# Attention's instructions queued behind the last product's eviction, and loads, splits and softmax given other priorities, in a hybrid encoder layer

## The chip, the cores and the metric

One core of one Trainium2 chip. The metric is the time of one execution in microseconds (us); three runs of the kernel before gave a median of 2874.46, from 2874.05 to 2876.97.

The core's engines each execute their own instructions in program order and wait for each other by semaphores: TensorE (PE; weight loads are listed apart as PEld), VectorE (DVE), ScalarE (ACT), GpSimd (POOL) and SyncE (SP). All loads and stores of this kernel are issued by SP, one after the other: an issue that has to wait, for its tile to come free or for the data that it stores, holds back every later issue.

## The reference

One layer on 2048 tokens of width 1024, in float32. Three mixers read the same normalised input; their outputs are projected, gated, added and projected again; an MLP follows.

```python
h = rmsnorm(x, g_mix)
z = h @ w_in                       # 1024 x 5648
qk_m, v_m, o_m, i_pre, f_pre, qkv_na, q_mem, gate_pre = jnp.split(z, split_idx, axis=-1)
...
h_m = ...    # bidirectional chunkwise mLSTM on qk_m (after a short convolution), v_m, gated by o_m
h_na = neighbourhood_attention(q_na, k_na, v_na, rpb)       # 8 heads, windows of 8 x 16 on a 32 x 64 grid
h_mem = memory_cross_attention(q_mem, rmsnorm(mem, g_mem), w_mem_kv, ...)   # 256 memory tokens, 4 heads
gates = jax.nn.sigmoid(gate_pre).reshape(bsz, s, 3, 1024)
y = gates[:, :, 0] * (h_m @ w_proj_mlstm) + gates[:, :, 1] * (h_na @ w_proj_na) \
    + gates[:, :, 2] * (h_mem @ w_proj_mem)
x = x + y @ w_out
return x + jnp.square(jax.nn.relu(rmsnorm(x, g_ffn) @ w_up)) @ w_down
```

Both attentions are a softmax over scores: the neighbourhood's scores get a bias (rpb) added, the memory's do not.

## The kernel before

**Products.** Every float32 operand of a large product is split in two parts, hi and lo, and each product is three matmuls, hi x hi, hi x lo and lo x hi (`mm3`, lines L240, L241 and L242). A product of 128 x 512 outputs over 1024 inputs is 8 x 3 = 24 matmuls into one PSUM bank (`tok_group` with tokens on the partitions, `ch_group` with channels there). ScalarE then moves the bank to SBUF; this is called the eviction here (L513, L528, L536, L548, L573, L616, L688 for the seven kinds of product). Phases 1 and 2 have two PSUM banks, tag `mm`, for products, so a product can begin only when the eviction of the one before the last is done. The attentions have three banks `tr` for transposes and three `mx` for scores and values.

**Phases.** Phase 1 goes over four blocks of 512 tokens (`block_a`). Each block computes q and k of the neighbourhood attention (`naqk`), q and k of the mLSTM, v of the neighbourhood attention and q of the memory attention (`navm`), v, for blocks 2 and 3 the 24 tiles of the branch gates, and o. At the end of block 3, hT, the split and normalised input, is loaded again with that of another block: three loads of a quarter (L580) and eight loads of parts of the last quarter (L584). Phase 2 uses it for the gates left over (`late_gates`, the first of them in two pieces, columns 0 to 383 and 384 to 511) beside the mLSTM. Phase 3 does the projections and the MLP.

**Streams.** Between the matmuls of a product, at every second step, `tick` runs one step of the jobs (transposes and splits of the next block's input, stores) and of each stream: the two attentions in phase 1, the mLSTM in phase 2. A step issues a handful of instructions: neighbourhood scores (L1094), bias and minimum (L1098), Exp (L1100), transposes (L1114) and their copies to npt (L1117 on ScalarE, L1119 on VectorE), values (L1128) and their split into nho (L1134, L1135); memory scores (L1246), maximum (L1249), Exp (L1253), transposes (L1265), copy to mpT (L1267).

**Order.** TensorE's order is as written in the program. On the other engines a scheduler picks, among the instructions whose inputs it takes to be ready, by priority: program order, shifted where the code changes `cur_priority`. A larger value goes later. Constants: LOW = 100, LATER = 60, SOON = 40. `issue_after(ins)` makes what is issued inside it come after `ins` in this order.

**Weights.** `fetch` loads a weight unit of 512 KB into one of three raw tiles (L181) and splits it, hi on ScalarE (L184) and lo on VectorE (L185), into one of five split tiles; all of it is shifted later by 60. Other loads and stores are issued at their place in the program: tiles of x (L473; two tiles, which the sums of w_down, L596, also use), q and k of the neighbourhood attention (L1048, L1049), its v (L1078, L1079), its bias (L1085, four tiles), stores (L105).

**Input.** `prep_x` scales a tile of the transposed input by eight VectorE instructions (L428), `split_part` splits it into hT (L445 on ScalarE, L446 on VectorE). In block 0 the input is transposed on TensorE and split at L361 and L362.

## Time and profile before

| what | value |
| --- | --- |
| median of three runs | 2874.46 us |
| profiled execution, its own time | 2875.37 us |
| its span in the trace | 2873.7 us |
| mean granted TensorE clock | 0.998 |
| TensorE waits in the span for neighbourhood scores, for memory Exps | 3.5 us, two times |
| TensorE wait for the first split input | 3.0 us, once |
| TensorE wait for an eviction of v | 1.8 us, once |
| DMA moved | 631.70 MB |

A row of a timeline has start in us, duration in us, engine, line, operation, output <- input by the program's names, shapes and types, count; in brackets the engine's idle time before it and what ended that. A row of the waits has the total in us, the number of waits, the longest. A row of the windows has the stretch, its length, the busy time of each engine asked for with its instructions in brackets, the granted clock (1.00 is full speed), the mean share of the DMA engines that is busy, and GB/s. In the rows of a window with all engines the order is PE, PEld, DVE, ACT, POOL.

### The profile page before, as it was taken

To read this page: it belongs to the slowest core of one execution; us is meant where nothing else is said; L and a number is where in the kernel's file an instruction comes from. 1 tells how busy PE (TensorE), PEld (TensorE's weight loads), DVE (VectorE), ACT (ScalarE), POOL (GpSimd) and SP (SyncE) were. 2 spreads that over 40 slices of the span, in tenths; PEclk is the share of its full clock that TensorE was granted. 3 is DMA by queue.
4 is the path that set the end of the run, shared out by engine and by line. 5 is a ranking of instruction groups with operands and counts; after the bars stand their busy time and mean duration, and the time that the engine had idled before them with its cause. 6 is when DMAs were issued, how large, how long until landed. Compare 5 with 4: busy or idle time off the path is not lost.

```text
span 2873.7 us, 41503 instructions
## 1 busy us (share of the span) xinstructions
PE 2852.6 (99%) x14950; PEld 2358.5 (82%) x14950; DVE 2042.3 (71%) x3518; ACT 1173.5 (41%) x2209; POOL 195.7 (7%) x254
## 2 busy tenths in 40 slices
PE   8999999999999999999999999999999999999999
PEld 7878788888888888888888888888788888888887
DVE  6676775577665545747699888866786998887666
ACT  7465654454544443532243334433312433343332
POOL 4121210011000112310000000000000000000000
PEclk9999999999999999999999999999999999999999
DMA  8686778877899888978444446756773444476553
GB/s 294 189 267 212 223 239 262 263 233 233 258 311 311 274 258 272 310 249 283 134 144 150 161 147 239 255 191 223 260 218 122 154 143 157 157 249 229 194 188 137
DMA packets 345149, 631.70 MB, mean 220 GB/s; under 512 B 29584, under 2 KB 151376, under 8 KB 344944
## 3 DMA queue, kind: packets, MB, share of 16 engines
q1 hardware_dynamic: 344944, 629.06, 66.8%
q8 instruction: 118, 1.93, 0.3%
q14 instruction: 87, 0.71, 0.1%
HBM read 452.32 MB, written 176.62 MB: 219 GB/s over the span
## 4 chain that ended last, share of the span: by engine, by line
PE 97%; DVE 1%; issue 1%; ACT 1%; DMA 0%; POOL 0%; SPq 0%; ACTq 0%; DVEq 0%; POOLq 0%
PE mm L240 29%; PE mm L242 29%; PE mm L241 29%; PE tr L1114 2%; PE mx L1128 1%; PE pn L890 1%; PE mx L1094 1%; PE pn L893 1%; PE mx L899 1%; PE mx L1275 1%; PE tr L1265 1%; PE mx L1246 0%; DVE ws L185 0%; PE mx L864 0%; PE tr L965 0%
## 5 line engine op out<-in xcount | busy, mean ns | idle before, releaser
L240 PE MATMUL mm<-X,ws 128*128 128x512 f32 x896 | 349.4, 390 | 0.0
L241 PE MATMUL mm<-X,ws 128*128 128x512 f32 x896 | 348.6, 389 | 0.0
L242 PE MATMUL mm<-X,ws 128*128 128x512 f32 x896 | 348.6, 389 | 0.0
L185 DVE TENSOR_TENSOR ws<-wr,ws 128x1024 fp32r<-128x1024 f32 (+2 forms) x195 | 238.9, 1231 | 133.9 <-ACT ws L184 131.8
L240 PE MATMUL mm<-hT,ws 128*128 128x512 f32 (+1 forms) x776 | 307.7, 397 | 0.7 <-ACT ev L573 0.7
L242 PE MATMUL mm<-hT,ws 128*128 128x512 f32 (+1 forms) x776 | 302.0, 389 | 0.0
L241 PE MATMUL mm<-hT,ws 128*128 128x512 f32 (+1 forms) x776 | 301.7, 389 | 0.0
L184 ACT ACTIVATE ws<-wr 128x1024 fp32r<-128x1024 f32 (+2 forms) x195 | 204.5, 1054 | 168.8 <-PE mm L242 116.3
L242 PE MATMUL mm<-X 128*128 128x512 f32 x616 | 239.7, 389 | 0.5 <-DVE X L1533 0.5
L240 PE MATMUL mm<-X 128*128 128x512 f32 x616 | 239.7, 389 | 0.1
L241 PE MATMUL mm<-X 128*128 128x512 f32 x616 | 239.6, 389 | 0.0
L240 PE MATMUL mm<-ws,hT 128*128 128x512 f32 (+2 forms) x640 | 232.9, 364 | 4.9 <-ACT hT L361 3.0
L210 ACT ACTIVATE ws<-wr 128x512 fp32r<-128x512 f32 x224 | 133.8, 627 | 232.4 <-PE mm L242 145.8
L242 PE MATMUL mm<-ws,hT 128*128 128x512 f32 (+2 forms) x640 | 224.9, 351 | 0.4 <-DVE hT L362 0.4
L241 PE MATMUL mm<-ws,hT 128*128 128x512 f32 (+2 forms) x640 | 224.2, 350 | 0.8 <-DVE ws L185 0.8
L1532 ACT ACTIVATE X<-X 128x1024 fp32r<-128x1024 f32 x109 | 115.7, 1062 | 213.4 <-DMA X<-s_s 96.0
L240 PEld LDWEIGHTS mm<-X,ws 128*128 128x128 f32 x896 | 168.2, 188 | 35.4 <-issue 0.5
L241 PEld LDWEIGHTS mm<-X,ws 128*128 128x128 f32 x896 | 168.2, 188 | 35.3 <-issue 0.5
L242 PEld LDWEIGHTS mm<-X,ws 128*128 128x128 f32 x896 | 168.2, 188 | 34.8
L1533 DVE TENSOR_TENSOR X<-X 128x1024 fp32r<-128x1024 f32 x109 | 132.1, 1222 | 62.1 <-ACT X L1532 61.5
L1549 DVE TENSOR_TENSOR acc<-acc,mm 128x512 f32<-128x512 f32 x192 | 126.3, 683 | 69.5 <-PE mm L242 69.4
L240 PEld LDWEIGHTS mm<-hT,ws 128*128 128x128 f32 x776 | 146.1, 188 | 31.6 <-issue 4.3
(280 smaller groups left out, 5953.6 us busy)
## 6 DMA issues: line engine op xcount, KB each, us to landing
wr<-in_w_units_dram SPq DMA_DIRECT2D x289, 512.0 KB
s_s<-u SPq DMA_DIRECT2D x32, 1024.0 KB
s_g<-ev SPq DMA_DIRECT2D x96, 256.0 KB
ev<-s_g SPq DMA_DIRECT2D x96, 256.0 KB
s_a<-u SPq DMA_DIRECT2D x96, 256.0 KB
X<-s_s SPq DMA_DIRECT2D x45, 512.0 KB
nab<-in_rpb_dram SPq DMA_DIRECT2D x96, 220.0 KB
xt<-in_w_units_dram SPq DMA_DIRECT2D x32, 512.0 KB
```

The costliest lines, as they stand in the source:

```text
L184: nc.scalar.activation(w[:, 0, ks], raw[:, ks], AF.Copy)
L185: nc.vector.tensor_tensor(w[:, 1, ks], raw[:, ks], w[:, 0, ks].bitcast(F32), ALU.subtract)
L210: nc.scalar.activation(hi, src, AF.Copy)
L240: mm(out, lhs[0], rhs[0], start=first, stop=False)
L241: mm(out, lhs[0], rhs[1], start=False, stop=False)
L242: mm(out, lhs[1], rhs[0], start=False, stop=last)
L890: mm(pn[h % 2][:, h // 2], pt[:, h], v1[:, h], start=h < 2, stop=first)
L893: mm(pn[h % 2][:, h // 2], qw[hp, h // 2], C[hp, h // 2], start=False, stop=True)
L1114: nc.tensor.transpose(ptp[0:120, j], sb[:, j * 120:(j + 1) * 120], self.ident)
L1532: nc.scalar.activation(hi, src, AF.Copy)
L1533: nc.vector.tensor_tensor(lo, src, hi.bitcast(F32), ALU.subtract)
L1549: nc.vector.tensor_tensor(c, first[t] if first else c, p, ALU.add)
```

## The change

Five edits, all on order:

- Each eviction is noted in `self.out`, and `tick` runs the streams inside `queued(self.out)`: what a stream issues comes after the last eviction written so far, on every engine that the scheduler orders. `behind`, used by the mLSTM, is now a call of the same helper.
- In `mem_unit` maximum and Exp are moved 40 earlier (`sooner()`).
- In `split_part` both halves of the split are moved 100 later (`sooner(-LOW)`).
- In `fetch` the load is issued at its place in the program; only the splits stay 60 later.
- The loads of q, k, v and bias of the neighbourhood attention are moved 100 earlier.

```diff
--- before.py
+++ after.py
@@ -89,7 +89,7 @@
         self.streams, self.qkq, self.memq, self.aux_end = [], [], [], False
         self.na_ready, self.na_end, self.na_rate, self.tk = [], False, 1, 0
         self.na_v, self.na_vfree = [], 2
-        self.jobs = []
+        self.jobs, self.out = [], ()
         self.wplan, self.wready = self.plan(), []
 
 
@@ -113,11 +113,12 @@
         f = self.jobs.pop(0) if self.jobs else None
         if f:
             f()
-        for g in list(self.streams):
-            try:
-                next(g)
-            except StopIteration:
-                self.streams.remove(g)
+        with self.queued(self.out):
+            for g in list(self.streams):
+                try:
+                    next(g)
+                except StopIteration:
+                    self.streams.remove(g)
         self.tk = (self.tk + 1) % 4
 
     def drain(self):
@@ -174,11 +175,11 @@
         w = w[:, :2 * n].rearrange("p (k l c) -> p l k c", k=nk, l=2)
         src = self.a["w_units"][i] if i < first else self.a["w_navm"][i - first]
         raw, src = (x.rearrange("p (k c) -> p k c", k=nk) for x in (raw, src))
-        prio = self.tc.cur_priority
-        self.tc.cur_priority = prio + self.later
         for k0 in range(0, nk, nk // parts):
             ks = slice(k0, k0 + nk // parts)
             nc.sync.dma_start(raw[:, ks], src[:, ks])
+        prio = self.tc.cur_priority
+        self.tc.cur_priority = prio + self.later
         for k0 in range(0, nk, nk // parts):
             ks = slice(k0, k0 + nk // parts)
             nc.scalar.activation(w[:, 0, ks], raw[:, ks], AF.Copy)
@@ -442,8 +443,9 @@
         nc = self.nc
         hi = dst[:, 0, 4 * g:4 * g + 4, t * 128:(t + 1) * 128]
         lo = dst[:, 1, 4 * g:4 * g + 4, t * 128:(t + 1) * 128]
-        nc.scalar.activation(hi, p, AF.Copy)
-        nc.vector.tensor_tensor(lo, p, hi.bitcast(F32), ALU.subtract)
+        with self.sooner(-LOW):
+            nc.scalar.activation(hi, p, AF.Copy)
+            nc.vector.tensor_tensor(lo, p, hi.bitcast(F32), ALU.subtract)
 
     def rms_x(self, b):
 
@@ -510,7 +512,7 @@
                 self.mem_rms()
             p = self.tok_group(hT, w, t)
             z = self.t("zna", [128, 512], 4)
-            nc.scalar.activation(z, p, AF.Copy)
+            self.out = nc.scalar.activation(z, p, AF.Copy).ins,
             self.qkq.append(self.na_qk(b, t, z.rearrange("p (a b) -> p a b", b=32)))
         if b + 1 < NB:
             rms = self.rms_x(b + 1)
@@ -525,7 +527,7 @@
         for t in range(4):
             p = self.tok_group(hT, w, t, slice(0, 256), 4)
             s = self.ev()[:, 0:256]
-            nc.scalar.activation(s, p, AF.Copy)
+            self.out = nc.scalar.activation(s, p, AF.Copy).ins,
 
             for half in range(2):
                 for r in range(2):
@@ -533,8 +535,8 @@
                     self.store(self.scr["vna"][half, 8 * b + 2 * t + r], s[p0:p0 + 40])
             p = self.tok_group(hT, w, t, slice(256, 528), 4)
             z = self.t("zm", [128, 256], 4)
-            nc.vector.tensor_copy(z, p[:, 0:256])
-            nc.scalar.activation(zif[:, t], p[:, 256:272], AF.Copy)
+            v = nc.vector.tensor_copy(z, p[:, 0:256])
+            self.out = v.ins, nc.scalar.activation(zif[:, t], p[:, 256:272], AF.Copy).ins
             self.memq.append(self.mem_unit(b, t, z))
         for g in {0: [0], 1: [1, 2], 2: [3, 4], 3: [5, 6, 7]}[b]:
             self.na_ready.append(g)
@@ -545,7 +547,7 @@
                 self.prep_x()
             p = self.tok_group(hT, w, t)
             s = self.ev()
-            nc.scalar.activation(s, p, AF.Copy)
+            self.out = nc.scalar.activation(s, p, AF.Copy).ins,
             self.store(self.scr["v"][b][t * 128:(t + 1) * 128], s)
             if b == NB - 1 and t % 2 == 0:
                 sums = sums or self.sums_down(15)
@@ -570,7 +572,7 @@
                 self.prep_x()
             p = self.tok_group(hT, w, t)
             s = self.ev()
-            nc.scalar.activation(s, p, AF.Tanh, scale=0.5)
+            self.out = nc.scalar.activation(s, p, AF.Tanh, scale=0.5).ins,
             nc.vector.scalar_tensor_tensor(s, s, 1.0, gml, ALU.add, ALU.mult)
             self.store(self.scr["og"][b][t * 128:(t + 1) * 128], s)
             if b == NB - 1:
@@ -613,7 +615,7 @@
 
         p = self.ch_group(w or self.take(1)[0], hT or self.hT, cuts)
         s = self.ev()
-        self.nc.scalar.activation(s, p, AF.Tanh, scale=0.5)
+        self.out = self.nc.scalar.activation(s, p, AF.Tanh, scale=0.5).ins,
         self.store(self.scr["gate"][b][j], s)
 
     def late_gates(self, more):
@@ -685,7 +687,7 @@
         self.n += 1
         z = self.p_a.tile([128, TB + 6], F32, name=f"cz_{self.n}", tag="cz", bufs=3)
         nc.vector.tensor_copy(z[:, 0:4], self.halo[:, c])
-        nc.scalar.activation(z[:, 4:4 + TB], p, AF.Copy)
+        self.out = nc.scalar.activation(z[:, 4:4 + TB], p, AF.Copy).ins,
         if last:
             nc.vector.memset(z[:, 4 + TB:], 0.0)
         else:
@@ -796,12 +798,22 @@
             self.rows[d, b] = dict(em=em, ac=ac)
 
     @contextlib.contextmanager
-    def behind(self):
+    def queued(self, marks):
 
         with contextlib.ExitStack() as stack:
-            for ins in self.marks:
+            for ins in marks:
                 stack.enter_context(self.tc.issue_after(ins))
             yield
+
+    def behind(self):
+        return self.queued(self.marks)
+
+    @contextlib.contextmanager
+    def sooner(self, n=SOON):
+
+        self.tc.cur_priority -= n
+        yield
+        self.tc.cur_priority += n
 
     def ml_chunk(self, d, c):
 
@@ -1043,10 +1055,11 @@
         qs = self.scr["qs"][:, g, hg].rearrange("(h d) l f t -> d h l (f t)", d=32)
         ks = self.scr["ks"][:, hg, :, kr0 * 64:(kr0 + nr) * 64].rearrange("(h d) l t -> d h l t", d=32)
 
-        for i, (lq, lk) in enumerate(((0, 0), (0, 1), (1, 0))):
-            ds = slice(32 * i, 32 * i + 32)
-            nc.sync.dma_start(q[ds].bitcast(F32), qs[:, :, lq])
-            nc.sync.dma_start(k[ds, :, :nr * 64].bitcast(F32), ks[:, :, lk])
+        with self.sooner(LOW):
+            for i, (lq, lk) in enumerate(((0, 0), (0, 1), (1, 0))):
+                ds = slice(32 * i, 32 * i + 32)
+                nc.sync.dma_start(q[ds].bitcast(F32), qs[:, :, lq])
+                nc.sync.dma_start(k[ds, :, :nr * 64].bitcast(F32), ks[:, :, lk])
         return q, k
 
     def na_unit(self, g, hg, half, before, wait):
@@ -1075,14 +1088,16 @@
         vt = self.p_a.tile([120, 4, 128], F32, name=f"nav{g}_{hg}_{half}", tag="nav", bufs=2)
         src = self.scr["vna"][half, kr0:kr0 + nr, :, hg * 128:(hg + 1) * 128].rearrange("r k c -> (r k) c")
         nf = nr // 3
-        nc.sync.dma_start(vt[:, :nf], src[:nf * 120].rearrange("(j p) c -> p j c", p=120))
-        nc.sync.dma_start(vt[:nr % 3 * 40, nf], src[nf * 120:])
+        with self.sooner(LOW):
+            nc.sync.dma_start(vt[:, :nf], src[:nf * 120].rearrange("(j p) c -> p j c", p=120))
+            nc.sync.dma_start(vt[:nr % 3 * 40, nf], src[nf * 120:])
         u["vt"] = vt
 
     def na_bias(self, u, h):
         bias = self.p_a.tile([128, 440], F32, name=f"nab{u['g']}_{u['hg']}_{u['half']}_{h}", tag="nab", bufs=NAB)
         pat = {0: 1, 7: 2}.get(u["g"], 0)
-        self.nc.sync.dma_start(bias[:, :u["nk"]], self.a["rpb"][pat, u["half"], u["hg"] * 4 + h, :, :u["nk"]])
+        with self.sooner(LOW):
+            self.nc.sync.dma_start(bias[:, :u["nk"]], self.a["rpb"][pat, u["half"], u["hg"] * 4 + h, :, :u["nk"]])
         u["bias"].append(bias)
 
     def na_scores(self, u, h):
@@ -1245,12 +1260,12 @@
                     js = slice(j * 64, j * 64 + 64)
                     nc.tensor.matmul(psc[j][:, p], q[js, lq, p], self.mk[js, lk, p], start=i == 0, stop=i == 2)
         for j in range(2):
-            nm = self.small(2, "m")
-            nc.vector.tensor_reduce(nm, psc[j], AX.X, ALU.max, negate=True)
-            sm = self.small(2, "m")
+            nm, sm = self.small(2, "m"), self.small(2, "m")
             e = self.t("me", [128, 2, 256], 4)
-            for p in range(2):
-                nc.scalar.activation(e[:, p], psc[j][:, p], AF.Exp, bias=nm[:, p:p + 1], accum_out=sm[:, p:p + 1])
+            with self.sooner():
+                nc.vector.tensor_reduce(nm, psc[j], AX.X, ALU.max, negate=True)
+                for p in range(2):
+                    nc.scalar.activation(e[:, p], psc[j][:, p], AF.Exp, bias=nm[:, p:p + 1], accum_out=sm[:, p:p + 1])
             rs = self.small(2, "m")
             nc.vector.reciprocal(rs, sm)
             nc.vector.tensor_tensor(e, e, rs.unsqueeze(2).to_broadcast([128, 2, 256]), ALU.mult)
```

How the order of instructions moves, at three places. A row is line, operation, output <- input, shape; x2 is a repeat. The line numbers of the changed kernel are up to 15 larger than those of before for the same instruction.

ScalarE at the third v product of block 0: me and sm are the memory softmax, mpT its transposed copy, nsb the neighbourhood scores, ev a product's tile for the store, mm its bank. Before:

```order
L608 ACTIVATE ev_152_1395<-tr_151_1390,bif_421 16x512
L1253 ACTIVATE me_157_1416,sm_156_1415<-mx_153_1399,sm_155_1413 128x256 x2
L1253 ACTIVATE me_161_1425,sm_160_1424<-mx_154_1400,sm_159_1422 128x256 x2
L1267 ACTIVATE mpT_167_1462<-tr_166_1457 128x512
L1100 ACTIVATE nsb1_429,sm_170_1486<-nsb1_429,sm_169_1484 128x320
L548 ACTIVATE ev_163_1437<-mm_150_1371 128x512
L548 ACTIVATE ev_172_1491<-mm_165_1450 128x512
```

Now:

```order
L1268 ACTIVATE me_157_1415,sm_156_1414<-mx_153_1399,sm_155_1413 128x256 x2
L1268 ACTIVATE me_161_1424,sm_160_1423<-mx_154_1400,sm_159_1422 128x256 x2
L550 ACTIVATE ev_163_1437<-mm_150_1371 128x512
L1282 ACTIVATE mpT_167_1462<-tr_166_1457 128x512
L1115 ACTIVATE nsb1_429,sm_170_1486<-nsb1_429,sm_169_1484 128x320
L185 ACTIVATE ws_131_1264<-wr_131_1263 128x2x512
L550 ACTIVATE ev_172_1491<-mm_165_1450 128x512
```

The eviction of mm_150 moved from behind the copy of mpT and the neighbourhood's Exp to ahead of both; the eviction of the next product, mm_165, stays behind them.

SP at the end of phase 1: the third load of a quarter of hT, the load of weight wr_1774 and the stores of the last o products. Before:

```order
L580 DMA hT_213<-s_hT1_157 128x16x128
L105 DMA s_o3_91<-ev_1779_10515 128x512
L580 DMA hT_213<-s_hT1_157 128x16x128
L105 DMA s_o3_91<-ev_1781_10545 128x512
L181 DMA wr_1774_10439<-in_w_units_dram 128x1024
L584 DMA hT_213<-s_hT1_157 128x2x128 x3
L105 DMA s_o3_91<-ev_1783_10575 128x512
L584 DMA hT_213<-s_hT1_157 128x2x128 x5
```

Now:

```order
L105 DMA s_o3_91<-ev_1779_10515 128x512
L582 DMA hT_213<-s_hT1_157 128x16x128
L180 DMA wr_1774_10439<-in_w_units_dram 128x1024
L105 DMA s_o3_91<-ev_1781_10545 128x512
L582 DMA hT_213<-s_hT1_157 128x16x128
L105 DMA s_o3_91<-ev_1783_10575 128x512
L586 DMA hT_213<-s_hT1_157 128x2x128 x8
```

The weight's load moved ahead of the third quarter of hT and of the store that preceded both; the eight part loads moved behind the last store.

VectorE at the gates of block 3: nho is the split of the neighbourhood's values, npt a copy of transposed scores, xt the tiles of the w_down sums, ws a weight's split. Before:

```order
L1135 TENSOR_TENSOR nho_1602_9547<-mx_1694_10015,nho_1602_9547 128x4x32
L1119 COPY npt_1696_10037<-tr_1695_10033 120x384
L1106 MEMSET nsb1_429 128x40
L1098 ISA nsb1_429,sm_1698_10041<-mx_1697_10039,nab7_1_0_0_9917 128x320
L1098 ISA sm_1698_10041 128x1
L185 TENSOR_TENSOR ws_1660_9822<-wr_1660_9821,ws_1660_9822 128x8x128
L1102 RECIPROCAL sm_1700_10045<-sm_1699_10043 128x1
L1103 TENSOR_SCALAR nsb1_429<-nsb1_429,sm_1700_10045 128x320
L1106 MEMSET nsb2_430 128x40
L1098 ISA nsb2_430,sm_1704_10071<-mx_1703_10069,nab7_1_0_1_9962 128x320
```

Now:

```order
L598 TENSOR_TENSOR xt_1659_9819<-xt_1659_9819,xt_1658_9817 128x512
L1134 COPY npt_1713_10110<-tr_1712_10106 120x384
L598 TENSOR_TENSOR xt_1659_9819<-xt_1659_9819 128x512
L1121 MEMSET nsb0_428 128x40
L598 TENSOR_TENSOR xt_1658_9817<-xt_1658_9817,xt_1659_9819 128x512
L598 TENSOR_TENSOR xt_1658_9817<-xt_1659_9819,xt_1658_9817 128x512
L186 TENSOR_TENSOR ws_1660_9822<-wr_1660_9821,ws_1660_9822 128x8x128
L1150 TENSOR_TENSOR nho_1602_9547<-mx_1694_10015,nho_1602_9547 128x4x32
L1113 ISA nsb2_430,sm_1704_10071<-mx_1703_10069,nab7_1_0_1_9962 128x320
```

The split of nho_1602 moved behind a copy that belongs to a later head, four sums of w_down and a weight's split; the scores' minimum of sm_1704 follows it as before. On ScalarE at the same place the Exp into sm_1705, which reads that minimum, now stands directly ahead of the gate's eviction ev_1707; before it stood behind it.

## The prediction

> **What bounds the kernel now.** I read the page's busy times and chain first, then the table of what TensorE waits for, then timelines around those waits.
>
> ```profile
> span 2873.7 us, 41503 instructions
> PE 2852.6 (99%) x14950; PEld 2358.5 (82%) x14950; DVE 2042.3 (71%) x3518; ACT 1173.5 (41%) x2209; POOL 195.7 (7%) x254
> PE 97%; DVE 1%; issue 1%; ACT 1%; DMA 0%; POOL 0%; SPq 0%; ACTq 0%; DVEq 0%; POOLq 0%
> ...
> PE mx L1094 <- ACT me L1253: 3.5, 2, 1.8
> PE mm L240 <- ACT hT L361: 3.0, 1, 3.0
> PE mm L240 <- ACT ev L548: 1.8, 1, 1.8
> ```
>
> TensorE is busy 99% of the span and 97% of the chain. The change leaves its instructions and their order alone, so the time can move only by TensorE's idle time (columns of the wait rows: us in total, times, longest) and by the clock that idling costs. What a reordering can win in phases 1 and 2 is mainly these waits, 8.3 us in all or 0.3%; what it can lose is not bounded by a row, since every wait that is hidden now can come out. So I took each wait and each place where the order of an in-order engine or of the one DMA queue (SP) changes, and asked who gets late. The profiled execution took 2875.37 us, 0.9 above the median 2874.46 of the three runs; I work out differences on its trace and add them to the median.
>
> **Term A, the eviction behind an attention Exp (gain).** Third v product of block 0:
>
> ```profile
> 124.80 0.56 ACT L1100 ACTIVATE nsb<-nsb,sm 128x320 f32<-128x320 f32 x1 [4.08 <-DVE sm L1098]
> 125.36 1.06 ACT L548 ACTIVATE ev<-mm 128x512 f32<-128x512 f32 x2
> ...
> 125.99 0.67 PE L240 MATMUL mm<-ws,hT 128*128 128x512 f32 x1 [1.76 <-ACT ev L548]
> ...
> 119.40:122.80 3.40, 3.40 (x19) 1.00 0.33 118
> 122.80:126.20 3.40, 1.64 (x8) 0.99 0.11 19
> 126.20:129.60 3.40, 3.40 (x11) 0.51 0.75 248
> ```
>
> ScalarE stood 4.08 us for the Exp's input while the eviction, ready long before, was queued behind it; the next matmul waited 1.76. Now the eviction stands ahead of the Exp (first order listing), so 1.8 goes. The window rows (length, TensorE busy with its matmuls, granted clock, DMA) show a second price: the 3.4 us after the stall ran at 0.51, 11 matmuls instead of 19, which loses 0.49 x 3.4 = 1.7. A = -3.4; bounds -1.8 (the clock would have dropped anyway) and -3.4.
>
> The Trainium skill, "TensorE: Matmul & The Clock Gate", section "Why this matters for your kernels", asks for no idle gap above about 3 us and says that one idle window brings half clock. By it the 1.76 us stall would have cost no clock, A would be -1.8 and the whole sum 1.7 slower; the row with 0.51 speaks against that.
>
> **Term B, memory Exps first (gain).** The two waits of L1094 for L1253 are the 3.5 us above. Ahead of the second one's Exps ScalarE had
>
> ```profile
> 312.41 0.60 ACT L513 ACTIVATE zna<-mm 128x512 f32<-128x512 f32 x1
> 312.90 0.59 ACT L1117 ACTIVATE npt<-tr 120x512 f32<-120x512 f32 x1
> 313.38 0.63 ACT L952 ACTIVATE sq<-zna 128x512 f32<-128x512 f32 x1
> ```
>
> 1.8 us that the Exps now precede, so nearly the whole wait (I take 1.6) can go. At the first, the reduction of the memory unit before it now stands on VectorE behind eight gain multiplications (2.2 us, term C) and a weight split (1.2), which can cost what the earlier Exps win; I count that wait as unchanged. B = -1.6; bounds -3.5 (both go) and 0.
>
> **Term C, the bias load ahead of stores (loss).** The o product of block 2, where SP must bring one weight in time:
>
> ```profile
> 582.62 0.62 DVE L1098 CUSTOM_DVE_ANT_0 nsb<-mx,nab 128x440 f32<-128x440 f32 x1 [1.49 <-PE mx L1094]
> ...
> 569.66 0.38 SPq L473 DMA_DIRECT2D xt<-in_xT_dram  x1
> 573.85 2.19 DVE L428 SCALAR_TENSOR_TENSOR xt<-xt,gmix,gbc 128x128 f32<-128x128 f32 x8 [0.92 <-DMA xt<-in_xT_dram]
> ...
> 584.94 0.43 SPq L181 DMA_DIRECT2D wr<-in_w_units_dram  x1
> 591.77 1.04 ACT L184 ACTIVATE ws<-wr 128x1024 fp32r<-128x1024 f32 x1
> 592.84 1.23 DVE L185 TENSOR_TENSOR ws<-wr,ws 128x1024 fp32r<-128x1024 f32 x1 [0.25 <-ACT ws L184]
> 594.12 0.50 PE L241 MATMUL mm<-ws,hT 128*128 128x512 f32 x1 [0.76 <-DVE ws L185]
> ```
>
> The bias nab4_0_0_0 takes the tile that the L1098 at 582.62 reads, so it cannot issue before 583.2. It now stands ahead of two s_t3 stores, an x tile that must wait until such a store has landed (two x tiles in all), and this weight's load. A transfer of that size took 4.2 us (569.66 to 573.85): 583.6 + 0.5 + 4.2 = 588.3 for the x tile, 588.7 for the weight, 3.7 later than 584.94. The weight had landed by 591.77; if it took between 4.2 and 6.8 us it lands between 592.9 and 595.5 now, and its two splits (2.27) end between 595.2 and 597.8, against 594.12. That is +1.1 to +3.7 beyond the 0.76 that is there. C = +2.2, near the middle; bounds 0 (the L1098 comes sooner) and +3.7.
>
> **Term D, low work ahead of a due operation (loss).** Gates of block 3:
>
> ```profile
> 878.71 0.49 PE L1114 MATMUL tr<-ident,nsb 128*120 128x128 f32 x3
> 879.70 0.55 DVE L1119 COPY npt<-tr 120x384 f32<-120x384 f32 x1
> L596 DVE TENSOR_TENSOR xt<-xt,xt 128x512 f32<-128x512 f32 x48 | 32.4, 685 | 14.5 <-DMA xt<-in_w_units_dram 14.0 <-issue 0.2
> 872.52 0.29 DVE L1135 TENSOR_TENSOR nho<-mx,nho 128x128 fp32r<-128x128 f32 x1 [1.93 <-ACT nho L1134]
> 876.18 0.49 DVE L1098 CUSTOM_DVE_ANT_0 nsb<-mx,nab 128x320 f32<-128x320 f32 x1
> ...
> 876.77 0.56 ACT L1100 ACTIVATE nsb<-nsb,sm 128x320 f32<-128x320 f32 x1
> 875.71 0.60 ACT L616 ACTIVATE ev<-mm 128x512 f32<-128x512 f32 x1 [0.68 <-PE mm L242]
> ...
> 882.16 0.40 PE L1094 MATMUL mx<-nak,naq 96*128 96x320 f32 x1
> 882.40 0.40 PE L240 MATMUL mm<-hT,ws 128*128 128x512 f32 x1
> ```
>
> In the new order (third listing) VectorE does the copy of npt_1713, which needs the transposes that end at 879.2, then three w_down sums (L596), the split of ws_1660, and only then L1135, which ran at 872.52 before. 879.2 + 0.5 + 3 x 0.65 + 1.2 + 0.3 = 883.1. TensorE's scores at 882.16 use the PSUM bank that L1135 frees: 1.0 late. Behind L1135 come L1098, the Exp and, on ScalarE behind that Exp, the eviction of ev_1707: 883.1 + 0.4 + 0.56 + 0.6 = 884.7, needed at 882.40 + 1.0 = 883.4, another 1.3. D = +2.3; bounds 1.0 (the first wait alone) and 2.8 (the copy at 879.70, as before).
>
> **Term E, the reload of the normalised input (loss).** Start of phase 2:
>
> ```profile
> 921.31 0.55 SPq L580 DMA_DIRECT2D hT<-s_hT  x1
> ...
> 926.75 0.53 SPq L580 DMA_DIRECT2D hT<-s_hT  x1
> ...
> 930.46 0.33 SPq L181 DMA_DIRECT2D wr<-in_w_units_dram  x1
> ...
> 926.00:927.00 1.00, 1.00 (x6) 0.82 (x5) 0.00 (x0) 0.24 (x1) 0.00 (x0) 1.00 0.72 264
> 927.00:928.00 1.00, 1.00 (x6) 0.83 (x5) 0.61 (x1) 0.36 (x1) 0.00 (x0) 1.00 0.02 8
> ...
> 932.85 0.44 PE L240 MATMUL mm<-hT,ws 128*128 128x384 f32 x1 [0.69 <-ACT ev L573]
> ...
> 30.60:34.00 3.40, 3.40 (x11) 0.50 0.85 324
> ```
>
> The DMA share falls from 0.72 to 0.02 at 927: the reload of 921.31 was done by 926.7, 5.4 us after its issue. The third reload was issued at 926.75. Now (second listing) it stands behind the load of wr_1774, which waits until a raw weight tile is free (issued 930.46, and nothing moves that earlier) and behind one store: issue at 931.2, done at 936.6. The first late gate multiplies columns 0 to 383, which this reload completes, from 932.16 (932.85 less its 0.69 wait): a wait of 4.4 in place of 0.69, +3.7. A shorter idle time cost 1.7 in half clock by term A's rows; two stretches at half clock, as at the start (the 30.60 row is the second), would cost 3.4. I take 2.5, between them. E = +6.2; bounds 0 (the raw tile is free 4 us sooner) and +7.1.
>
> **Term F, loads behind weights that wait (loss).**
>
> ```profile
> SPq L181 <- DVE ws L185: 110.3, 62, 9.9
> ```
>
> A weight's issue stood on SP 1.8 us on the mean (110.3 / 62) until a split had freed its tile. At the start four weight loads now precede two tiles of x, and their splits come earlier; the 3.0 us wait for L361 becomes several smaller ones. I take half a mean wait, +0.9, bounds -3.0 and +3.0. The keys of the neighbourhood attention's groups 6 and 7 also come to stand behind a waiting issue, half a mean wait each less some slack: +1.0, bounds 0 and +2.
>
> **Priced at nothing.** Low splits of the input (L445, L446) and later stores: the two eviction tiles come free later, but the eviction is due one product of 24 matmuls later, 24 x 3.4 / 19 = 4.3 us, and takes 0.6; if that cover went, each store 1 us too late would cost 1 us. Phase 3 keeps its order.
>
> Sum: -3.4 - 1.6 + 2.2 + 2.3 + 6.2 + 0.9 + 1.0 = +7.6; 2874.46 + 7.6 = **2882 us**, 0.26% slower. About 0.2%, 5.7 us, is what a measurement of this kernel can tell from no change.
>
> **Rivals.** (1) *Early weights carry the rest* (faster). Loads that leave SP earlier bring splits earlier; C, E and the start's 3.0 us wait vanish, D keeps 1.0 without its split, B gives 2.6 with no split before the reduction: -3.4 - 2.6 + 1.0 + 1.0 - 3.0 = -7.0, 2867.5. For: 110.3 us of SP waiting for splits. Against: raw tiles are freed at the pace of the products, which stays. It decides if wr_1774 issues before 926.3, so that the reload behind it lands in time. (2) *Transfers land sooner than they did*, in 3 us instead of 5.4: C is 0, E's wait 1.3 without half clock: 7.6 - 2.2 - 2.4 - 2.5 = +0.5, 2875. For: a DMA share of 0.02 at 927, so the engines have time. Against: the 4.2 us of term C for half the bytes. (3) *Half clock in more places*: C and D cost 1.7 each as well, +11.0, 2885.5. For: 1.76 us of idling was enough at 126. Against, around the two waits of term B:
>
> ```profile
> 172.00:175.50 3.50, 3.20 (x16) 1.00 0.92 208
> ```
>
> the clock stayed at 1.00 (the smaller of the two waits, 3.5 - 1.8 = 1.7, lies at its start). (4) *The clock falls only after a whole idle stretch of the length of these windows*: A is -1.8, 2883.7; the 0.51 row is against it. (5) *It does not do what it says*: an operation is put behind the eviction of the product before it alone, so ev_1707 still stands behind an Exp; were that so at A too, 2885.5. The first listing speaks against it.
>
> **Numbers.** Forecast 0.41 (2879 to 2885), rivals 1 to 5: 0.14, 0.22, 0.15, 0.04, 0.04. The range 2872 to 2888 leaves out rival 1 and some of rival 3; all low bounds together would give 2866, all high ones 2891. Faster by over 0.2% (below 2868.7): 0.10, most of rival 1. Within: 0.04 of rival 1, rival 2 and the 0.05 of the forecast below 2880.2, 0.31. Slower: 0.36 of the forecast and rivals 3 to 5, 0.59.
>
> **What would show it.** A and B: no wait of L240 for L548's eviction in block 0, none of L1094 for the memory Exps near 313. C: a wait near 592 of 2 us or more. D: two waits near 882, of the scores and of the gate's first matmul. E: the first 128x384 matmul of the late gates waiting about 4 us for the reload, with a clock of about 0.5 behind it. The forecast is wrong if SP issues the third reload before 928, or if TensorE's idle time in phase 1 does not grow.

## The result, and the profile after

| kernel | median us | lowest to highest | runs |
| --- | --- | --- | --- |
| before | 2875.84 | 2874.05 to 2879.00 | 6 |
| the change | 2893.78 | 2890.20 to 2899.76 | 6 |

The ratio is 1.0065, interval 1.0054 to 1.0076: 18 us slower, where 2882 (2872 to 2888) was forecast. The sign was right, the size less than half of what came. The profiled execution of the change took 2899.76 us, the slowest of its six, so the places below add up to some 6 us more than the medians differ by.

The page's span, busy times and chain of the changed kernel, and its table of TensorE's waits (us in total, times, longest):

```profile
span 2898.0 us, 41514 instructions
PE 2859.4 (99%) x14950; PEld 2361.9 (81%) x14950; DVE 2042.2 (70%) x3518; ACT 1169.7 (40%) x2209; POOL 195.2 (7%) x254
PE 91%; DMA 4%; DVE 2%; issue 1%; ACT 1%; SPq 0%; POOL 0%; DVEq 0%; ACTq 0%; POOLq 0%
...
PE mm L241 <- DMA s_o<-ev: 7.1, 1, 7.1
PE mm L241 <- ACT hT L362: 3.7, 3, 2.8
PE mm L241 <- ACT ws L185: 3.3, 1, 3.3
PE mm L241 <- ACT ev L618: 2.6, 3, 1.2
PE mx L1109 <- DMA nab<-in_rpb_dram: 2.4, 1, 2.4
PE mx L1109 <- ACT me L1268: 2.3, 2, 2.1
PE mx L1261 <- ACT me L1268: 2.0, 2, 1.0
PE mx L1109 <- DVE nho L1150: 1.8, 1, 1.8
```

TensorE did not work in 2898.0 - 2859.4 = 38.6 us, against 21.1 before: 17.5 of the 24.3 us by which the profiled span grew. The other 6.8 are busy time, most of it the same matmuls at half clock: 24.5 us of this trace ran at 0.50, against 13.7 before. The wait for an eviction of v (L548 before, L550 now) is gone. The largest wait is put down to a store of o, but what the matmul needed was the reload of hT behind it on SP, as term E below shows. The wait put down to a bias (nab) is one for keys, as the part on the keys below shows. The windows of the changed kernel around the four places with long waits (stretch, length, TensorE busy with its matmuls, clock, DMA):

```profile
593.46:596.87 3.41, 0.61 (x2) 1.00 1.04 382
596.87:600.28 3.41, 3.41 (x17) 0.50 0.95 356
849.46:852.87 3.41, 1.09 (x5) 1.00 1.03 304
852.87:856.28 3.41, 3.41 (x9) 0.50 0.97 351
893.83:897.24 3.41, 1.72 (x7) 1.00 0.84 286
897.24:900.66 3.42, 3.42 (x16) 0.50 0.85 194
948.44:951.86 3.42, 0.00 (x0) 1.00 1.04 353
951.86:955.27 3.41, 0.85 (x3) 0.50 1.13 357
955.27:958.68 3.41, 3.41 (x12) 0.50 1.04 336
```

Each of these waits is followed by a stretch at 0.50, and the edges of these stretches lie on one grid: 3.413 us apart, from 593.46 to 955.27 a whole number of steps (106). One long wait is not: the 2.1 us for a memory Exp at 169. There the grid cuts the idle time in two, 1.03 and 1.07 us:

```profile
166.79:170.21 3.42, 2.38 (x33) 1.00 0.68 254
170.21:173.62 3.41, 2.35 (x13) 1.00 0.95 265
```

Where the 24.3 us came in, by the start of the same matmul in both traces (TensorE's order is the same), idle time and half clock apart:

| place (time before) | term | forecast | idle | half clock | sum |
| --- | --- | --- | --- | --- | --- |
| start to 95 | F | +0.9 | not split | not split | +0.7 |
| 126 | A | -3.4 | -1.8 | -1.6 | -3.4 |
| 167 to 172, 309 to 316 | B | -1.6 | +2.1 | | +2.1 |
| 593 | C | +2.2 | +3.2 | +1.5 | +4.7 |
| 767, 844 | keys | +1.0 | +3.4 | +1.6 | +5.0 |
| 876 to 885 | D | +2.3 | +4.4 | +1.7 | +6.1 |
| 932 | E | +6.2 | +6.4 | +1.8 | +8.2 |
| 1050 and later | | 0 | +1.0 | | +1.0 |
| sum | | +7.6 | +18.7 | +5.0 | +24.4 |

The split into idle and half clock is by the steps at a wait and in the 3.4 us behind it; the page's busy time draws the line 2 us elsewhere. The start is not split because the two traces differ there in both: two stretches at half clock against three before, and more idle time. Of the 5.0 at 767 and 844, 0.7 came in at 767, ahead of a matmul of the memory scores and not of one that reads keys.

### The profile page after: what moved, and what is told of

Same layout as the page of the kernel before. It is cut to its first block, busy times and chain, and to the rows that moved or that the text cites. A ratio compares the mean times of both kernels' runs of the same rounds, so it can differ in the third digit from the quotient of the medians.

```text
span 2898.0 us, 41514 instructions
## 1 busy us (share of the span) xinstructions
PE 2859.4 (99%) x14950; PEld 2361.9 (81%) x14950; DVE 2042.2 (70%) x3518; ACT 1169.7 (40%) x2209; POOL 195.2 (7%) x254
## 4 chain that ended last, share of the span: by engine, by line
PE 91%; DMA 4%; DVE 2%; issue 1%; ACT 1%; SPq 0%; POOL 0%; DVEq 0%; ACTq 0%; POOLq 0%
PE mm L241 28%; PE mm L243 27%; PE mm L242 27%; PE tr L1129 2%; PE pn L902 1%; PE mx L1143 1%; PE mx L1109 1%; DMA nab<-in_rpb_dram 1%; DMA wr<-in_w_units_dram 1%; DMA X<-s_hm 1%; PE pn L905 1%; PE mx L911 1%; DVE ws L186 1%; PE mx L1290 1%; PE tr L1280 0%
```

## The experiments

Fifteen kernels ran. The runs of one group ran on the same chip beside the kernel before, and ratios are to that.

### First group: which edits cost the time

**Without the last edit.** The five edits but that on the attention's loads:

```diff
-        with self.sooner(LOW):
+        with self.sooner(0):       # q and k, v, bias: all three places
```

> The whole change but for its last edit: the loads of the neighbourhood attention's q, k, v and bias stay at their place. Theory T1 (these loads, moved ahead of stores, wait for their tiles on SP and push everything behind them later, down to the reload at the start of phase 2): the third reload of hT is issued ahead of wr_1774 again, the wait of about 7 us at the start of phase 2 falls below 1 us, and the time is 2873 to 2882 us. Theory T2 (the weight loads, issued 60 steps earlier, are what holds the reload back, as the prediction had it): the wait of 6 to 7 us stays and the time is 2887 to 2896 us.

Measured: 2881.96 us, ratio 1.0023 (1.0013 to 1.0032). The wait at the start of phase 2 is gone. A new one came in, at 644, where weight loads stand ahead of a key load:

```profile
PE mx L1109 <- DMA nak<-s_ks: 7.5, 1, 7.5
```

The time is at the upper end of T1's range. T1 holds for the reload and T2 falls. Two thirds of the 18 us hang on the last edit.

**The last edit alone**, on the kernel before.

```diff
+        with self.sooner(LOW):
             nc.sync.dma_start(...)   # q and k, v, bias of the neighbourhood attention
```

> Before with the last edit alone: the loads of the neighbourhood attention 100 earlier. T1: the wait at the start of phase 2 (4 us or more) and one near 592 of 3 us or more appear though no weight load was moved, 2888 to 2898 us; the 1.8 us wait for the eviction near 125 stays. T2: no wait over 2 us at the start of phase 2, 2874 to 2880 us.

Measured: 2900.50 us, ratio 1.0089 (1.0073 to 1.0104), above the range that T1 gave and 24 us slower than before.

```profile
PE mm L241 <- DMA hT<-s_hT: 5.7, 1, 5.7
PE mm L241 <- ACT ws L185: 4.6, 1, 4.6
PE mm L241 <- ACT ev L618: 3.4, 2, 2.7
PE mx L1109 <- DVE nho L1150: 3.1, 2, 1.7
PE mm L241 <- ACT ev L550: 1.8, 1, 1.8
```

Terms E, C and D are all here, with not one weight load moved: T1. The interval just touches that of the whole change (1.0054 to 1.0076), so it is likely, and not shown, that the other four edits took some of the loss back.

T1 says that these loads wait for their tiles on SP. SP's own waits show it: a bias load waits until the minimum of the scores (L1098 before, L1113 now) has read the tile that it is to fill. The row before, then that of the whole change (us, times, longest):

```profile
SPq L1085 <- DVE sm L1098: 66.0, 46, 7.3
SPq L1100 <- DVE sm L1113: 150.0, 58, 8.4
```

In the run of the last edit alone it is 166.2 us, in the one without the last edit 36.6.

**Weight loads alone at their place.**

```diff
-        prio = self.tc.cur_priority
-        self.tc.cur_priority = prio + self.later
         for k0 in range(0, nk, nk // parts):
             ...
             nc.sync.dma_start(raw[:, ks], src[:, ks])
+        prio = self.tc.cur_priority
+        self.tc.cur_priority = prio + self.later
```

> Before with the weight loads alone issued at their place in the program. T1: no wait over 1 us at the start of phase 2; some waits of about 1 us elsewhere in phase 1, 2876 to 2884 us. T2: the wait of 4 us or more at the start of phase 2 is there, 2884 to 2892 us.

Measured: 2884.72 us, ratio 1.0023 (1.0013 to 1.0034). No wait over 0.7 us at the start of phase 2, as T1 has it; the time is just above T1's range, at the lower end of T2's. It goes in waits of 0.4 to 1.8 us at 52 to 58, 167 (with half clock behind it), 620 to 690, 873 and 1115. The wait at 126 is gone in this run too, though no stream is queued behind an eviction in it.

**No loads moved:** queueing, softmax and low splits together.

```diff
 fetch: the load shifted later again, as before
-        with self.sooner(LOW):
+        with self.sooner(0):       # all three places
```

> The change without both edits on loads: queueing behind the eviction, memory softmax first, low input splits. T1 and T2: the wait of 1.8 us at 125 and the half clock behind it are gone (-3.4), no wait at the start of phase 2 over 1 us, 2869 to 2874 us. A third theory, T3 (the queueing itself puts an Exp or a low operation ahead of what is due, as at 882): waits of 1 to 3 us in blocks 1 to 3 stay, 2877 us or more.

Measured: 2881.35 us, ratio 1.0018 (1.0009 to 1.0027): slower than before. The wait at 126 and its half clock are gone, 3.4 us, but at 166 TensorE waits 2.3 us for a memory Exp. ScalarE there:

```profile
164.18 1.06 ACT L457 ACTIVATE xt<-xt 128x1024 f32<-128x1024 f32 x1 [2.21 <-DMA xt<-in_x_dram]
165.23 0.46 ACT L1268 ACTIVATE me<-mx,sm 128x256 f32<-128x256 f32 x1
```

ScalarE stands 2.21 us for a tile of the next block's x, which it is to square, with the Exp behind it: the same kind of stall as the one that the change removes, on another operation. At 592 the wait for a weight's split is 3.9, and at 878 keys come 1.7 us late; each of the three is followed by half clock. Against before, the profiled run loses 2.4 us at 166, 5.2 at 592 and 3.4 at 878. T3's time came, but by these places, not by the one at 882.

### Second group: what a removed wait is worth

**One eviction.** Before, with the streams queued only in the v products of block 0; ScalarE's order changes at three positions.

```diff
+        with self.queued(self.out if self.blk == 0 and self.inv else ()):   # inv: in the v products
             for g in list(self.streams):
```

> Before, but with the streams queued behind the last eviction only during the v products of block 0: ScalarE's order changes at three positions there, no other engine's does. Theory T4 (an edit is worth what its row says as long as SP's order stays): the wait of 1.8 us at 125 and the half clock behind it go and nothing else changes, -3.4 us, 2872 to 2873 us beside a before of 2875 to 2876. Theory T5 (the freed time is taken back at the next wait): a longer wait at 172 and the time of before, within 1 us.

Measured: 2876.24 us, ratio 1.0000 (0.9991 to 1.0008). By 130 the profiled run was 4.5 us ahead of the kernel before, 1.3 of them from the start and 3.2 from here; by 873 it was 3.6 behind. Its waits, and two of its grid's stretches with what follows them:

```profile
PE mx L1112 <- ACT me L1271: 3.4, 2, 1.8
PE mx L1112 <- DMA nak<-s_ks: 1.9, 1, 1.9
PE mx L1112 <- DVE nsb L1124: 1.4, 1, 1.4
...
164.57:167.98 3.41, 1.82 (x31) 1.00 0.61 210
167.98:171.40 3.42, 3.42 (x12) 0.50 0.95 277
311.35:314.76 3.41, 1.57 (x10) 1.00 0.98 358
314.76:318.18 3.42, 3.42 (x12) 0.50 1.03 299
```

The two memory Exp waits are as long as before, but now both halve the clock, and at 844 and 872, where the kernel before had no wait, keys come late. T5 in its result, though no longer wait at 172 made it.

**Two waits.** The same and the memory softmax first in block 1.

```diff
-            with self.sooner(0):
+            with self.sooner(SOON if b == 1 else 0):
                 nc.vector.tensor_reduce(nm, psc[j], AX.X, ALU.max, negate=True)
```

> The kernel of the run before with the memory softmax 40 earlier in block 1 alone, which moves two places of SP. T4: the wait at 314 falls by 1.6 us as well, -5.0 us against before, 2870 to 2872 us, faster than both kernels. T5: 2874 to 2876 us.

Measured: 2874.75 us, ratio 0.9994 (0.9985 to 1.0002): in T5's range and above T4's. The wait at 314 is gone as expected, and the profiled run is 4.8 us ahead of the kernel before by 316; at 872 it loses 4.0 again, 2.5 to the keys and the rest to half clock.

**Queueing alone, in all blocks.**

```diff
+        with self.queued(self.out):
             for g in list(self.streams):
```

> Before with only the streams queued behind the last eviction, in all blocks. SP's order changes in some 170 places through it (stores and tiles of x for the w_down sums). T4: the 1.8 us wait at 125 is gone, but waits near 592 or 872 of 1.5 us or more come in, 2875 to 2882 us. T5 and the prediction's pricing (the edit costs nothing elsewhere): 2871 to 2873 us.

Measured: 2876.30 us, ratio 1.0000 (0.9990 to 1.0009), from 2872.29 to 2880.30: the time that T4 gave without its waits of 1.5 us. Those near 618 and 873 cost 1.0 and 0.6 us in the profiled run, which was one of the shortest. What the longer runs waited for is not known.

**Made stalls**, for the clock. Before every second late gate VectorE adds zero times the last product to part of the weight, so that TensorE must wait.

```diff
+STALLS = [(512, 256), (512, 512), (512, 384), (512, 512, 128)]
 ...
+        for n in STALLS[self.ng // 2 % len(STALLS)]:
+            hi = w[:, 0, 0:n // 128]
+            last = self.lastp[:, 0:n].rearrange("p (k c) -> p k c", c=128)
+            self.nc.vector.scalar_tensor_tensor(hi, last, 0.0, hi.bitcast(F32), ALU.mult, ALU.add)
```

> Before with 24 made stalls in phase 2: ahead of every second late gate VectorE adds zero times the last product to part of the weight, two or three times, so that TensorE idles some 1.3 to 2.5 us each time; some 45 us of idling in all. Theory G1 (the clock is set for each stretch of a fixed grid of 3.41 us by how much of the stretch before was idle, with a limit near 1.7 us): stalls of the same length of about 2 us sometimes halve the clock for the next 3.41 us and sometimes not, by whether they lie in one stretch or across two. Theory G2 (the length of an idle time decides alone): all stalls above some length halve it and none below. With half of them halving the clock at 1.6 us each, 2930 to 2950 us by G1; G2 2920 or 2960 us.

Measured: 2922.22 us, one run; TensorE waited ten times for them, 24.8 us in all, not 24 times, so the total tells nothing between the theories. The windows on its grid say more:

```profile
121.84:125.26 3.42, 2.01 (x10) 1.00 0.01 3
125.26:128.67 3.41, 3.06 (x15) 1.00 0.76 245
```

This is the very stall of term A, 1.76 us at the same matmul. In the kernel before it lay in one stretch of the grid and halved the clock; here the grid happened to cut it in 1.41 and 0.35, and the clock stayed at 1.00. That alone does not decide, for the same stall lay whole in one stretch in two more traces, that of the last edit alone (1.76) and that of the softmax edit alone (1.73), and the clock stayed at 1.00 there too. The first of them:

```profile
122.76:126.17 3.41, 1.65 (x9) 1.00 0.07 7
126.17:129.58 3.41, 3.41 (x17) 1.00 0.79 244
```

Longer waits decide. The 2.1 us at 169 of the changed kernel and 2.24 us at 166 in the softmax edit alone, each cut in two pieces of at most 1.2, left the clock at 1.00; 2.26 us in one stretch, in the run with no loads moved, halved it:

```profile
163.94:167.35 3.41, 1.15 (x13) 1.00 0.82 332
167.35:170.77 3.42, 3.42 (x15) 0.50 0.59 157
```

So the length of a wait does not decide by itself, and G1 holds in that the idle time of one stretch counts; its single limit near 1.7 does not. Counted over the traces of this kernel and of its variants, from 40 us on, stretches at full clock: of 34 with 1.0 to 1.55 us idle none was followed by half clock, of 31 with 1.55 to 2.0 us 17 were, of 19 with more than 2.0 us all were. The largest of the 31 that did not halve it had 1.94 us idle (a made stall), the smallest that did 1.59; what decides among these stays open.

### Third group: the stretch where the DMA engines are full

In block 3's gates the kernel before has no wait, but its DMA engines are nearly always busy:

```profile
800.00:850.00 50.00, 50.00 (x341) 1.00 0.99 314
850.00:900.00 50.00, 50.00 (x334) 1.00 0.96 314
```

Three kernels load and split 12 of block 3's 24 gate weights and use each twice, 6 MB less; half of that block's gates are then computed with another gate's weight. With the bytes go twelve issues on SP and the twelve splits on ScalarE and VectorE, so these runs cannot tell the bytes from those.

```diff
-                out += u["gate"]
+                out += u["gate"][::2] if b == NB - 1 else u["gate"]
 ...
-                self.gate(b, j)
+                if b < NB - 1 or j % 2 == 0:
+                    gw, = self.take(1)
+                self.gate(b, j, gw)
```

> Before, but block 3 loads and splits only 12 of its 24 gate weights and uses each for two gates (half of its gates are computed with the wrong weight), 6 MB less at 314 GB/s in the stretch from 790 to 920 whose DMA engines are 97% busy. It is the base for the two runs beside it. Theory D1 (the stretch is bound by transfers in about half of the executions, which is the spread of 2873 to 2880 of the kernel before): the spread narrows and the median falls by 1 to 3 us, 2872 to 2875. Theory D2 (transfers there cost nothing): 2874 to 2877, with the spread of before.

> The kernel of run e6 (two waits taken away) with the same fewer bytes. D1 (what is won ahead of the stretch is waited for again inside it, at the keys of 844 and 872): with the bytes gone the whole gain of the two waits arrives, 3.5 to 5 us below the base beside it. D2 (the gain is lost elsewhere, by the clock): 1 to 2.5 us below the base.

> The whole change with the same fewer bytes. D1: the wait for a bias near 848 and those near 890 to 895 shrink below 1 us and with them their half clocks, so 6 to 10 us below the whole change, 2884 to 2888; the wait of 7 us at the start of phase 2 stays. D2 (the order of SP and VectorE alone makes them): 2890 or more.

Measured:

| kernel, fewer bytes | median us | lowest to highest | ratio to before |
| --- | --- | --- | --- |
| before | 2874.69 | 2873.64 to 2878.22 | 0.9992 (0.9983 to 1.0001) |
| two waits | 2872.27 | 2871.20 to 2873.62 | 0.9983 (0.9974 to 0.9992) |
| the change | 2883.87 | 2880.30 to 2886.80 | 1.0024 (1.0014 to 1.0034) |

The kernel before lies in both ranges, and its interval reaches 1.0001: nothing is told by it. The two waits are worth 2.4 us on that base, short of D1's 3.5 to 5 and at the upper end of D2's; no wait for keys is left in the profiled run, and its runs lie within 2.4 us, where those of the two waits with all bytes spread over 5.5. In that trace the wait at 172 halves the clock, 1.5 us. With all bytes the two waits were worth 2.2 us by the medians, so that the full stretch takes back part of a gain rests on the profiled run with its late keys at 872 alone; the medians do not show it. The whole change gains 10 us by fewer bytes, a time just under D1's range: the wait of 2.4 us for keys at 849 is gone, as D1 says, while D's two waits stay (0.7 and 1.2, with half clock) and C's is 4.2. E, which D1 had left in place, is gone too, but there SP has the third reload ahead of the weight in this kernel, so that part is the order's and not the bytes'.

**The softmax edit alone.**

```diff
+            with self.sooner():
                 nc.vector.tensor_reduce(nm, psc[j], AX.X, ALU.max, negate=True)
```

> Before with the memory softmax 40 earlier as the only edit. Theory S1 (maximum and Exp, moved ahead in the order of priority, come to stand behind a square of the next block's x that waits for its load, as at 164 in run e4): a wait of 1.5 to 2.5 us at 166 to 168 in place of the one at 172, the one at 314 smaller, 2876 to 2881 us. Theory S2, the prediction's: both waits shrink and none comes in, 2873 to 2875 us.

Measured: 2884.18 us, ratio 1.0028 (1.0018 to 1.0038). S1's waits are there. The time is above S1's range, and at 592 there is a wait that S1 did not have:

```profile
PE mm L241 <- ACT ws L185: 4.3, 1, 4.3
PE mx L1261 <- ACT me L1268: 4.2, 2, 2.2
```

The wait for the Exps moved from the neighbourhood's scores (L1094 before) to the memory's own (L1261), and grew. Moving two kinds of operation by 40 steps also changed SP's order in some 250 places, and the weight at 592 came late.

### Fourth group: what was still open

**Early attention loads in blocks 0 to 2 only.**

```diff
-        with self.sooner(LOW):
+        with self.sooner(LOW if self.blk < 3 else 0):
```

> The whole change, but in block 3 the loads of the neighbourhood attention stay at their place; in blocks 0 to 2 they are early as in the change. Theory K1 (early key and bias loads in block 3 alone, where the DMA engines are 96 to 99% busy, make the waits at 849, 894 and 948 and their half clocks, 18 of the 24 us of the profiled run): the third reload is ahead of the weight again, no wait over 1 us at the start of phase 2, the wait at 594 stays, 2876 to 2883 us. Theory K2 (the order that SP has by then from the earlier blocks makes them): 2888 to 2894 us.

Measured: 2884.51 us, ratio 1.0021 (1.0010 to 1.0033). SP at the end of phase 1 has the third reload ahead of the weight, and no wait over 1 us follows:

```profile
935.20 0.52 SPq L582 DMA_DIRECT2D hT<-s_hT  x1
...
938.91 0.34 SPq L180 DMA_DIRECT2D wr<-in_w_units_dram  x1
```

K1: without the early loads of block 3 the waits at 849, 894 and 948 are gone, and none over 0.7 us is left between 600 and 1000. That those loads alone would make them was not run. The wait at 594 stays, and grew from 3.3 to 4.4 us with two stretches at half clock behind it in place of one; the time is 1.5 us above the expected range.

**The whole change without the softmax edit.**

```diff
-            with self.sooner():
+            with self.sooner(0):
                 nc.vector.tensor_reduce(nm, psc[j], AX.X, ALU.max, negate=True)
```

> The whole change without the memory softmax first. Beside the other edits this changes two places of VectorE's order and none of SP's. Theory M1 (within the whole change the edit does nothing, so the two Exp waits near 165 and 171 are there without it): 2890 to 2897 us, with 2 to 3 us of waits for L1268 between 160 and 172. Theory M2 (it costs what it costs alone in run e12, 8 us): 2883 to 2888 us.

Measured: 2898.32 us, ratio 1.0071 (1.0057 to 1.0085), the whole change's ratio within the intervals, though above M1's range. M1: inside the whole change this edit makes no difference that can be measured, while alone it cost 8 us; the edits do not add up. The waits for Exps are there without it.

**Three waits: a try at a faster kernel.** Queueing in the v products of block 0, softmax first in block 1, splits low in blocks 0 and 1.

```diff
+        with self.queued(self.out if self.blk == 0 and self.inv else ()):
 ...
+            with self.sooner(SOON if b == 1 else 0):                  # maximum and Exp
 ...
+        with self.sooner(-LOW if self.blk <= 1 else 0):               # split_part
```

> A try at a kernel that beats both: before with the streams queued behind the eviction in the v products of block 0, the memory softmax first in block 1, the input splits low in blocks 0 and 1. SP's order changes in 75 places of blocks 0 and 1. Theory T4: the waits at 125, 172 and 314 fall by 4 us together and, as in run e10, part of it is waited for again at the keys of 844 and 872: 2871 to 2874 us. Theory R (any change of SP's order ahead of block 2 comes out at 592): a wait of 2.5 us or more at 592, 2876 us or more.

Measured: 2872.10 us (2870.33 to 2873.26, 11 runs), ratio 0.9981 (0.9973 to 0.9990): faster than both kernels. No wait of TensorE between 100 and 1000 us is over 0.8 us, and 1.0 us is left of those for memory Exps. T4. The waits at 126, 172 and 314 are gone, 6.0 us by 316 in the profiled run with the half clock of the first, and 1.7 of them come back at 613 and 868. The low splits alone were not run.

## Why the prediction was right or wrong

**Direction and bound.** TensorE's waits and clock alone made the time, as said; slower was right. The range was not: 2893.78 lies above 2888, and above the 2891 that all the high bounds make together. Three steps failed: that nothing else stands ahead of B's Exps; that C, D and the keys cost idle time alone, without the half clock behind it (4.8 of the 16.8 us missing); and that the reload and the keys would land as fast as in the kernel before. The edit that makes D and E was named wrongly or not at all.

**A** was right to the tenth: -1.8 idle, -1.6 clock. The mechanism of the idle part is shown by the run that moves three positions of ScalarE. The clock part was luck: five traces have this stall (before, the last edit alone, the softmax edit alone, the made stalls, before with fewer bytes), and only in the first of them did it halve the clock. -1.8 was as fair a number, and an average over executions lies between.

**The rule on the gate.** The prediction set the Trainium skill's sentence on gaps above about 3 us against the 0.51 row. The runs bear the row out: stretches with 1.59 to 1.99 us idle halved the clock 17 times. The Trainium skill, "TensorE: Matmul & The Clock Gate", section "What's actually happening", describes a free-running window of 3413 ns and puts half clock behind a whole idle window. The stretches on the 3.413 us grid agree with the window; the limit here is near half of it idle, between 1.55 and 2.0 us.

**B** failed in its sign, +2.1 for -1.6. At the second place (314) the three operations are out of the way and the wait did shrink, from 1.8 to 0.2, the 1.6 of the forecast. The step that failed is that nothing else would stand ahead of the Exps. At 309, a few us earlier, new waits of 1.6 us came in, 1.0 of them for an Exp, and the place ends 0.5 behind. At the first place a square of the next block's x (L457) stands ahead of an Exp, and ScalarE waits there for its load:

```profile
168.13 1.06 ACT L457 ACTIVATE xt<-xt 128x1024 f32<-128x1024 f32 x1 [2.67 <-DMA xt<-in_x_dram]
```

The prediction counted that wait as unchanged; it went from 1.67 to 3.1 together with the one ahead of it. ScalarE stood 2.51 us for the same kind of load at 301 to 304, ahead of the new waits at 309; that these come from it was not tested. That the edit itself makes no measurable difference in the whole change (run without it: ratio 1.0071) was not seen either.

**C** was right in its chain, SP's bias, stores, x tile and weight. SP stood 3.1 us for the bias's tile, until 582.72:

```profile
582.73 0.35 SPq L1100 DMA_DIRECT2D nab<-in_rpb_dram  x1
583.14 0.94 SPq L105 DMA_DIRECT2D s_t<-xt  x2
588.94 0.34 SPq L475 DMA_DIRECT2D xt<-in_xT_dram  x1
589.34 0.42 SPq L180 DMA_DIRECT2D wr<-in_w_units_dram  x1
```

The weight was to issue at 588.7 and issued at 589.34. The wait grew by 3.2, inside the bounds; the 1.5 of half clock behind it was left out. The place is sensitive to other edits as well: with no loads moved it waits 3.9 us, with the softmax edit alone 4.3.

**D** was right in both waits and what each stood for (1.8 for L1150, 1.2 for the eviction behind the Exp), forecast 1.0 and 1.3. The error is size: one more wait before it and the half clock, 6.1 for 2.3. The prediction named the low operations of VectorE and no edit; the runs name the early attention loads, since both waits are there with these alone (1.7 and 2.7) and gone without those of block 3.

**The keys** of group 7 came 2.4 us late, with half clock behind it, for a forecast of 1.0. The table puts this wait down to a bias, which the matmul does not read. By the semaphore times in the trace the last load of its keys, issued at 840.89, had landed at 851.64, and the matmul began at 851.78. That load took 10.8 us; in the kernel before the same one took 6.1 (837.00 to 843.12). SP was held up there by landings too: its issues at 846.12, 850.47 and 851.66 each came 0.01 to 0.02 us after the landing of the issue eight places ahead, whose semaphore they use again.

**E** came as described: the reload stood behind the weight on SP.

```profile
945.62 0.55 SPq L180 DMA_DIRECT2D wr<-in_w_units_dram  x1
946.23 0.42 SPq L105 DMA_DIRECT2D s_o<-ev  x1
946.75 0.53 SPq L582 DMA_DIRECT2D hT<-s_hT  x1
...
954.42 0.66 PE L241 MATMUL mm<-hT,ws 128*128 128x384 f32 x1 [7.10 <-DMA s_o<-ev]
```

The issue, at 946.75, is as forecast (931.2 and the shift of 15.2 by then make 946.4). The mis-sized term is the transfer, 7.7 us from issue to use (landed after 7.4) where the prediction took 5.4 from the kernel before, whose own third reload landed after 5.3: +6.4 idle for +3.7. Half clock cost 1.8 for 2.5. The cause was put in the wrong edit: not the weight loads (alone: no such wait) but the attention's loads (alone: 5.7 us), those of block 3.

**Where the 16.8 us between 7.6 and 24.4 are:** half clock at C, at the keys and at D 4.8, B 3.7, idle at the keys 2.4, at D 2.1, at C 1.0, E 2.0, phases 2 and 3 1.0, F -0.2. The waits of the forecast and the mechanism of rival 3, half clock in more places, were both right: they were set beside each other as cases with chances, when the first brings the second. Rivals 1, 2, 4 and 5 fell. Rival 2's argument, free DMA engines at 927, was the opposite of what the stretch from 800 to 900 is.

**The bounds.** Each loss was priced by its own rows at the load on the queues that the kernel before had there. Where one thing comes late on a full queue, transfers lengthen and idle times pass the limit of the gate, and the terms behind it err to the same side. The low and high bounds had been treated as if they could offset each other, and five terms passed their own high bound in the profiled run: B (+2.1 for 0 at most), C (4.7 for 3.7), D (6.1 for 2.8), E (8.2 for 7.1) and the keys (5.0 for 2).

## What to carry to other kernels

Moving an issue forward on an in-order queue is no gain by itself: if its tile is not free yet, everything behind it waits (SP stood 150 us for bias tiles in place of 66), and on this kernel the damage came out up to a phase later. Change the smallest set of positions that removes a named wait, and compare the whole order of every queue: the same ideas, kept to two blocks (75 places of SP's order), gained 5 us and applied everywhere lost 18. Idle time of a TensorE that is otherwise full should be priced with a chance of half clock behind it, from about 1.6 us on in one stretch of the grid.

## What the runs showed of the hardware

- The granted clock changes only at points of a 3.413 us grid. A stretch with more than 2.0 us idle was followed by 3.41 us at 0.50 in 19 of 19 cases, one with 1.0 to 1.55 in 0 of 34, and of 31 between these 17 were. The same 1.76 us stall cost 1.7 us of clock in one execution and nothing in four others, in two of which it also lay in one stretch. The position of the grid against the program differs between executions; this is likely part of why equal executions of the kernel before lie between 2873.2 and 2883.8 us, but that was not measured by itself.
- A reload of 1 MB landed 5.3 us after its issue in the kernel before (926.75 to 932.05) and 7.4 in the changed one (946.75 to 954.18), where DMA shares were 1.04 to 1.13. A load of keys landed after 6.1 and after 10.8 us.
- From 800 to 900 us the DMA engines are 96 to 99% busy with TensorE never idle: in other runs one late load of keys there cost 1.7 us (no loads moved), 2.4 (the change) and 2.5 (two waits) of waiting.
